# A hybrid decoder layer: in the MLP's second products, the adding transfers for product 6's weights are issued ahead of those for product 5's

## The chip, the cores and the metric

The kernel runs on one core of a Trainium2 chip. The metric is the device time of one execution in microseconds (us). The core has TensorE (PE) for matrix products, VectorE (DVE), ScalarE (ACT) and GpSimd (POOL) for the rest, and SyncE (SP), which issues transfers. Sixteen DMA engines carry out all transfers. Those that SyncE issues (queue q1) are plain copies here; those that GpSimd issues (queue q0) can add what they read to what already stands in the destination.

## The reference, cut to what matters

One decoder layer on 512 tokens of width 1024: two token mixers side by side (windowed attention and a convolution module), and behind them an MLP. The change lies in the MLP alone:

```python
hmid = jnp.square(jax.nn.relu(rms_norm(x, norm_mlp_g[l]) @ w_ff1[l]))   # 512 x 1024 @ 1024 x 4096
x = x + hmid @ w_ff2[l]                                                  # 512 x 4096 @ 4096 x 1024
```

Inputs and outputs are float32.

## The kernel before, in words

The 4096 hidden units are cut into four quarters of 1024. Each quarter has a stage of first products (the normed input by a quarter of `w_ff1`) and a stage of second products (the squared result by a quarter of `w_ff2`), so the MLP has eight stages, `ph` 0 to 7, and the second products are the odd ones. In the profile they begin at 478.66, 557.30, 633.61 and 709.92 us.

A stage multiplies 2 x 2 blocks by a scheme with seven block products in place of eight, numbered 1 to 7. In a second stage TensorE takes them in the order 1, 7, 6, 2, 5, 4, 3 (`ORDER`). Each is 24 matmuls (L1190) into the bank `ps_z`, `ps_y` or `ps_x`: products 1, 6, 5 and 3 go to `ps_z`, 7 and 4 to `ps_y`, 2 to `ps_x`.

The weights of a product are a 512 x 512 block, or a sum or difference of blocks. They come in two halves (`h` 0 and 1) of 256 rows, 512 KB each, and each half goes through these steps:

- `fetch` (L1128): a plain transfer on SyncE's queue into one of four buffers, `block0` to `block3`.
- `piece_hi` (L1153): ScalarE rounds the half to a high piece, `pieceh`.
- `piece_lo` (L1156): VectorE subtracts that from the half, which gives the low piece, `piecel`. A product is high by high, high by low and low by high, three matmuls for each tile. There are four pieces of each kind, used in turn.
- `fetch_add` (L1132): some products need the block of an earlier product plus another block. Once both pieces of a half have been made, GpSimd issues a transfer that adds the other block into the same buffer. In a second stage product 5's weights are product 1's plus a block (buffer `h11`), product 6's are product 7's plus a block (buffer `ht`), and product 4's are product 6's plus another (again `ht`). That makes six adding transfers in a stage.

`row_add` (L1195) on VectorE adds the finished bank to the running output, and `op_hi` (L1224), `op_lo` (L1228) and `op_sum` (L1233 to L1238) make the operands from the squared result.

The order on each engine is written out by hand: `at(pos, fn, ...)` gives every step a position, all steps are sorted by it, and each engine and each queue works through its own part in that order. The positions count in units of a quarter of a product, from `m`, the start of a stage. A position sets the order alone; when a step runs is set by what it waits for.

Of the kernel before, what the change touches and what calls it, by code (L numbers as in the profile page):

```python
# [53 lines left out]
def tile_hybrid_block(  # L54
# [295 lines left out]
    def at(pos, fn, *args):  # L350
        events.append((pos, len(events), fn, args))
# [755 lines left out]
    def homes(ph):  # L1107


        w, x, y, z = 0, 1, 2, 3  # L1110
        for _ in range(ph // 2):
            w, x, y, z = y, w, z, x
        return (w, x, y, z) if ph % 2 == 0 else (w, z, x, x)

    def home(ph, prod):
        return homes(ph)[{1: 0, 5: 0, 7: 1, 6: 1, 4: 1, 3: 2, 2: 3}[prod]]
# [51 lines left out]
    def halves(ph, j, t):  # L1168

        return [slice(c, c + 256) for c in (0, 256)] if (ph, j, t) == (PHASES - 1, 6, 1) else [slice(0, S)]  # L1170
# [115 lines left out]
    for ph in range(PHASES):  # L1286
        m = M0 + 28 * ph
        order = ORDER[ph]
        ff1 = ph % 2 == 0
        h11, ht, h22, h21 = homes(ph)  # L1290
# [18 lines left out]
        for j, prod in enumerate(order):  # L1309
            p = m + 4 * j  # L1310
            for h in range(2):
                n = 2 * (7 * ph + j) + h
                s, lo = p - 5.9 + 2 * h, 0.75
                if ph == 0 and j < 2:
                    s, lo = ((W0 + 5.6, 0.75), (W0 + 8.2, 0.75), (W0 + 21.8, 1.1), (W0 + 22.6, 4.5))[n]
                elif ph == 0 and (prod, h) == (5, 1):
                    lo = 0.85
                elif ph == 0 and (prod, h) == (4, 0):
                    s = p - 4.88
                elif ph == 0 and (prod, h) == (4, 1):  # L1320
                    s = p - 3.8
                elif not ff1 and prod == 7:
                    s = m - 2.95 + 2 * h
                elif not ff1 and prod == 6:
                    s = p - 3.4 + 2 * h
                at(s, piece_hi, n, home(ph, prod), h)
                at(s + lo, piece_lo, n, home(ph, prod), h)
                for t in range(2):
                    for cols in halves(ph, j, t) if h else (slice(0, S),):
                        at(p + 2 * h + t, products, ph, prod, n, h, t, cols)  # L1330
                d = s + 0.9
                if ff1:
                    if prod == 5:
                        at(d, fetch, ph + 1, h11, 0, 0, h)
                    elif prod == 4:
                        at(d, fetch, ph + 1, ht, 1, 0, h)
                elif prod == 1:
                    at(d, fetch_add, ph, h11, 0, 1, h)
                elif prod == 7:
                    at(d, fetch_add, ph, ht, 0, 0, h)  # L1340
                elif prod == 6:
                    at(d, fetch_add, ph, ht, 1, 0, h)
                elif prod == 2:
                    at(d, fetch, ph, h21, 1, 1, h)
                elif ph + 1 < PHASES:
                    at(d, fetch, ph + 1, home(ph, prod), *{5: (0, 1), 4: (1, 1), 3: (1, 0)}[prod], h)
            for t in range(2):
                e = p + 3.1 + t
                if ff1:
                    if prod in (1, 7, 6):  # L1350
                        at(e, c_copy, {1: 0, 7: 3, 6: 2}[prod], ph, prod, t)
                    elif prod == 3:
                        at(e, relu_of, 1, ph, prod, t, -1.0)
                    else:
                        at(e, c_add, {2: 0, 5: 3, 4: 2}[prod], ph, prod, t)
                else:
                    half_t, half_n, minus, store = {1: (0, 0, 0, 0), 7: (1, 1, 1, 0), 6: (1, 0, 0, 0), 2: (0, 0, 0, 1),
                                                    5: (1, 1, 1, 1), 4: (1, 0, 0, 1), 3: (0, 1, 1, 1)}[prod]
                    for part in halves(ph, j, t):
                        at(e, row_add, ph, half_t, half_n, prod, t, minus, store, part)  # L1360
            if ff1 and prod in (2, 5, 4):
                i, scale = {2: (0, 1.0), 5: (3, -1.0), 4: (2, 1.0)}[prod]
                late = 7.6 if ph == 0 and prod == 2 else 0
                at(p + (5.1 if prod == 4 else 4.9) + late, relu, i, scale)
                at(p + 5.5 + late, square_of, i)
            elif ff1 and prod == 3:
                at(p + 4.8, square_of, 1)
# [200 lines left out]
```

## Time and profile before

| what | value |
|---|---|
| median of 3 runs | 754.54 us (753.19 to 754.95) |
| the profiled execution's own time | 754.11 us |
| its span, first to last instruction | 752.3 us |
| TensorE busy | 744.9 us, 99% of the span |
| VectorE, ScalarE, GpSimd busy | 611.8, 445.0, 270.2 us |
| granted TensorE clock | 1.0 |
| adding transfers on GpSimd (L1132) | 34 of 512 KB, median 8.4 us from issue to landing |
| plain transfers of MLP weights on SyncE (L1128) | 64 of 512 KB, median 6.0 us |

A row of the timeline gives start, duration, engine, line, operation, the tile written and the tiles read, the count of merged instructions (x), and in brackets how long the engine stood idle before it and what ended that. A row of the stage windows gives the stretch, its length, then the busy time of PE, PEld (weight load), DVE, ACT and POOL, each with its count of instructions, the granted clock, the mean busy share of the DMA engines and GB/s. The chain of waits is the work that ended last, followed back from the end; its rows are start, duration and what. DMA lines give a queue's packets, MB and the time of its packets as a share of the sixteen engines' time in that stretch.

### The profile page before, as it was taken

The numbers are of one execution on the slowest core, as the hardware profiler recorded it, in microseconds if no ns is written. First come the engines' busy times: TensorE is split into PE (matmuls) and PEld (weight loads), VectorE is DVE, ScalarE is ACT, GpSimd is POOL, SyncE is SP. The second block draws the span as 40 slices with busy tenths as digits, with TensorE's granted clock in tenths as the row PEclk, the third lists the DMA queues.
The fourth block names the chain that finished last, engine by engine and source line by source line (L and its number), as shares of the span: only waits on it lengthen the run. The fifth ranks groups of instructions, "written<-read, shape, count | busy, mean of one in ns | idle before, by whom it ended". The sixth has DMA issues, their size and how long they took to land.

```text
span 752.3 us, 11423 instructions
## 1 busy us (share of the span) xinstructions
PE 744.9 (99%) x4338; PEld 652.9 (87%) x4338; DVE 611.8 (81%) x935; ACT 445.0 (59%) x709; POOL 270.2 (36%) x213
## 2 busy tenths in 40 slices
PE   8999999999999999999999999999999999999998
PEld 7889998898888888888888899978998899889986
DVE  7939998889978888878347679899779977998786
ACT  7645467667576656348225467764675467646751
POOL 0365788948666555534440002210121012101210
PEclk9999999999999999999999999999999999999999
DMA  8521131304132131623319107972598359834772
GB/s 321 196 98 43 56 114 57 109 33 140 56 124 75 57 104 65 213 68 112 111 59 332 59 29 132 247 198 96 149 215 202 108 138 218 197 121 116 171 162 112
DMA packets 64903, 97.99 MB, mean 130 GB/s; under 512 B 3104, under 2 KB 34384, under 8 KB 64848
## 3 DMA queue, kind: packets, MB, share of 16 engines
q1 hardware_dynamic: 55600, 79.44, 31.3%
q0 software_dynamic: 9248, 17.83, 13.5%
q8 instruction: 34, 0.56, 0.3%
q14 instruction: 21, 0.17, 0.1%
HBM read 95.13 MB, written 2.12 MB: 129 GB/s over the span
## 4 chain that ended last, share of the span: by engine, by line
PE 92%; DMA 3%; DVE 2%; issue 1%; ACT 1%; POOL 0%; SPq 0%; DVEq 0%; POOLq 0%; ACTq 0%
PE ps_z L1190 11%; PE ps_x L1185 9%; PE ps_y L1190 5%; PE ps_y L1185 4%; PE ps_x L1190 3%; PE ps_kv L1386 3%; PE ps_z L1185 2%; PE ps_g L502 2%; PE ps_q L192 2%; DMA block<-in_w_ff_dram 2%; PE ps_q L194 2%; PE ps_q L193 2%; PE ps_a L502 2%; PE ps_ta L502 2%; PE ps_g L504 2%; PE ps_a L504 2%
## 5 line engine op out<-in xcount | busy, mean ns | idle before, releaser
L1153 ACT CAST pieceh<-block 128x1024 fp32r<-128x1024 f32 x112 | 115.8, 1049 | 75.4 <-DMA block<-in_w_ff_dram 19.9
L1156 DVE TENSOR_TENSOR piecel<-block,pieceh 128x1024 fp32r<-128x1024 f32 x112 | 135.6, 1219 | 27.7 <-ACT pieceh L1153 27.6
L811 DVE SCALAR_TENSOR_TENSOR cv<-h,wcol,cv 128x512 f32<-128x512 f32 x208 | 146.1, 746 | 0.5
L1132 POOL DMA_DIRECT2D block<-in_w_ff_dram x34 | 41.4, 1248 | 290.7 <-DMA block<-in_w_ff_dram 148.3
L1185 PE MATMUL ps_x<-xSh,pieceh 128*128 128x256 f32 x192 | 53.0, 276 | 0.0
L1185 PE MATMUL ps_x<-xSl,pieceh 128*128 128x256 f32 x192 | 53.0, 276 | 0.0
L1185 PE MATMUL ps_x<-xSh,piecel 128*128 128x256 f32 x192 | 53.0, 276 | 0.0
L719 ACT ACTIVATE s<-s,negm 128x257 f32<-128x257 f32 (+1 forms) x64 | 30.4, 478 | 15.8 <-DVE negm L711 15.8
L1190 PE MATMUL ps_z<-piecel,aSh 128*128 128x512 f32 (+1 forms) x98 | 38.2, 390 | 1.0 <-DVE piecel L1156 1.0
L1190 PE MATMUL ps_z<-pieceh,aSh 128*128 128x512 f32 (+1 forms) x98 | 37.9, 386 | 0.4 <-ACT pieceh L1153 0.4
L1190 PE MATMUL ps_z<-pieceh,aSl 128*128 128x512 f32 (+1 forms) x98 | 37.7, 385 | 0.0
L1146 DVE TENSOR_TENSOR block<-block,block 128x1024 f32<-128x1024 f32 x30 | 36.5, 1221 | 0.8 <-DMA block<-in_w_ff_dram 0.4
L192 PE MATMUL ps_q<-wh_q,uTh 128*128 128x256 f32 x128 | 36.5, 286 | 0.0
L803 POOL TENSOR_TENSOR side<-side,tap 128x512 f32<-128x512 f32 x24 | 31.1, 1296 | 15.1 <-ACT tap L802 15.1
L194 PE MATMUL ps_q<-wh_q,uTl 128*128 128x256 f32 x128 | 36.2, 283 | 0.0
L193 PE MATMUL ps_q<-wl_q,uTh 128*128 128x256 f32 x128 | 36.2, 283 | 0.0
L1185 PEld LDWEIGHTS ps_x<-xSh,pieceh 128*128 128x128 f32 x192 | 36.0, 188 | 0.0
L1185 PEld LDWEIGHTS ps_x<-xSl,pieceh 128*128 128x128 f32 x192 | 36.0, 188 | 0.0
L1185 PEld LDWEIGHTS ps_x<-xSh,piecel 128*128 128x128 f32 x192 | 36.0, 188 | 0.0
L743 DVE TENSOR_TENSOR pTl<-ptp,pTh 128x512 fp32r<-128x512 f32 x28 | 19.1, 687 | 18.0 <-ACT pTh L739 18.0
L728 POOL TENSOR_TENSOR s<-s,r 128x1024 f32<-128x1024 f32 (+1 forms) x16 | 26.9, 1684 | 16.5 <-DVE r L723 16.5
L1224 ACT CAST aSh<-c 128x1024 fp32r<-128x1024 f32 x16 | 16.9, 1053 | 22.7 <-DVE c L1238 11.4
(332 smaller groups left out, 2501.6 us busy)
## 6 DMA issues: line engine op xcount, KB each, us to landing
block<-in_w_ff_dram SPq DMA_DIRECT2D x64, 512.0 KB, 6.0
block<-in_w_ff_dram POOLq DMA_DIRECT2D x34, 512.0 KB, 8.4
raw_g<-in_w_in_dram SPq DMA_DIRECT2D x8, 512.0 KB, 4.5
raw_a<-in_w_in_dram SPq DMA_DIRECT2D x8, 512.0 KB, 4.4
raw_q<-in_w_in_dram SPq DMA_DIRECT2D x8, 512.0 KB, 4.0
raw_ta<-in_w_in_dram SPq DMA_DIRECT2D x8, 512.0 KB, 3.9
raw_tc<-in_w_in_dram SPq DMA_DIRECT2D x8, 512.0 KB, 3.9
raw_wo<-in_w_attn_o_dram SPq DMA_DIRECT2D x8, 512.0 KB, 4.0
```

The source lines that it names most:

```text
L192: pe.matmul(ps, ah, wh, start=first, stop=False)
L193: pe.matmul(ps, ah, wl, start=False, stop=False)
L194: pe.matmul(ps, al, wh, start=False, stop=last)
L502: pe.matmul(ps, wh[:, k, :], ah(k), start=(k == 0), stop=False)
L803: ge.tensor_tensor(out=side[ct], in0=side[ct], in1=tap, op=ALU.add)
L811: ve.scalar_tensor_tensor(out=cps[ct], in0=src, scalar=w, in1=cps[ct], op0=ALU.mult, op1=ALU.add)
L1132: ge.dma_start(tl["raw"][buf][:, ks, :], block(ph, i, j)[:, ks, :], accum_op=ALU.add)
L1146: ve.tensor_tensor(out=o, in0=a, in1=b, op=ALU.add)
L1153: se.copy(piece("h", n), tl["raw"][buf][:, 2 * h:2 * h + 2, :])
L1156: ve.tensor_tensor(out=piece("l", n), in0=tl["raw"][buf][:, 2 * h:2 * h + 2, :], in1=piece("h", n).bitcast(F32), op=ALU.subtract)
L1185: pe.matmul(o, b[:, c, w], a[:, k, :], start=(first and c + q + i == 0), stop=(k == 3 and i == 2), skip_group_check=True)
L1190: pe.matmul(acc[:, cols], a[:, k, w], b[:, c, cols], start=(first and c + i == 0), stop=(k == 3 and i == 2), skip_group_check=True)
```

## The change

One position is another. Before, the adds for product 5 (called at product 1, half 0 and 1) stood 0.9 units behind the cast of product 1's half, at `m - 5.0` and `m - 3.0`; those for product 6 (called at product 7) stand at `m - 2.05` and `m - 0.05`, and those for product 4 (called at product 6) at `m + 5.5` and `m + 7.5`. Now product 5's stand at `m + 1.0` and `m + 1.05`.

```diff
                 elif prod == 1:
-                    at(d, fetch_add, ph, h11, 0, 1, h)
+                    at(m + 1.0 + 0.05 * h, fetch_add, ph, h11, 0, 1, h)
                 elif prod == 7:
                     at(d, fetch_add, ph, ht, 0, 0, h)
                 elif prod == 6:
                     at(d, fetch_add, ph, ht, 1, 0, h)
```

GpSimd in the first quarter's second stage, before (-) and after (+). Here `block0` is `h11` (product 1's and then 5's) and `block3` is `ht` (product 7's, then 6's, then 4's); DMASW and DMAHW are the semaphores of GpSimd's and SyncE's transfers.

```order
-L1132 DMA block0_4026<-in_w_ff2_dram 128x2x512 [waits DMAHW1_49,DVE_49]
-L1132 DMA block0_4026<-in_w_ff2_dram 128x2x512 [waits DMAHW2_49,DVE_49]
 L1132 DMA block3_4137<-in_w_ff2_dram 128x2x512 [waits DMASW2_49,DVE_49]
 L1132 DMA block3_4137<-in_w_ff2_dram 128x2x512 [waits DMASW3_49,DVE_49]
-L1132 DMA block3_4137<-in_w_ff2_dram 128x2x512 [waits DMASW6_49,DMASW0_49,DVE_49]
-L1132 DMA block3_4137<-in_w_ff2_dram 128x2x512 [waits DMASW7_49,DMASW1_49,DVE_49]
+L1132 DMA block0_4026<-in_w_ff2_dram 128x2x512 [waits DMAHW1_49]
+L1132 DMA block0_4026<-in_w_ff2_dram 128x2x512 [waits DMAHW2_49]
+L1132 DMA block3_4137<-in_w_ff2_dram 128x2x512 [waits DMASW4_49,DMASW0_49,DVE_49]
+L1132 DMA block3_4137<-in_w_ff2_dram 128x2x512 [waits DMASW5_49,DMASW1_49,DVE_49]
```

Product 5's two stood first and now stand third and fourth; product 6's two go from third and fourth to the front, and product 4's two stay fifth and sixth. The wait of product 5's adds for VectorE is gone, since what they wait for lies ahead of what product 6's wait for.

VectorE in the same stage, where it makes the low pieces of products 6 (`block3`), 2 (`block1`) and 5 (`block0`):

```order
 L1195 TENSOR_TENSOR x_1_3377<-x_1_3377,ps_z_4355 128x512 [waits PE_49]
-L1156 TENSOR_TENSOR piecel_4154<-block_4137,pieceh_4153 128x1024 [waits DMASW6_49,Activation_49]
+L1156 TENSOR_TENSOR piecel_4154<-block_4137,pieceh_4153 128x1024 [waits DMASW4_49,Activation_49]
 L1156 TENSOR_TENSOR piecel<-block_4027,pieceh 128x1024 [waits DMAHW3_49,Activation_49]
 L1195 TENSOR_TENSOR x_2_3379<-x_2_3379,ps_y_4352 128x512 [waits PE_49]
-L1156 TENSOR_TENSOR piecel_4176<-block_4137,pieceh_4175 128x1024 [waits DMASW7_49,Activation_49]
+L1156 TENSOR_TENSOR piecel_4176<-block_4137,pieceh_4175 128x1024 [waits DMASW5_49,Activation_49]
```

No instruction of VectorE moves; only the semaphores are others, since the transfers' numbers follow their order of issue. The same holds for ScalarE and SyncE, and TensorE's order is unchanged.

## The prediction

> **What bounds the kernel now.** I read the page's engine line first, then TensorE's waits, the chain of waits, the stage windows, and last the transfers behind the one wait that the chain shows.
>
> ```profile
> span 752.3 us, 11423 instructions
> PE 744.9 (99%) x4338; PEld 652.9 (87%) x4338; DVE 611.8 (81%) x935; ACT 445.0 (59%) x709; POOL 270.2 (36%) x213
> ...
> PE ps_z L1190 <- DVE piecel L1156: 1.0, 2, 0.8
> PE ps_z L1190 <- ACT pieceh L1153: 0.4, 1, 0.4
> ```
>
> TensorE is busy 99% of the span, so a change of the order of transfers can gain only where TensorE waits. From 478 us on its only waits are these two lines: matmuls of the second products (L1190) that wait for a weight piece. The next two views show where. The chain is in order of time (start, us, what).
>
> ```profile
> 483.30 9.00 DMA block<-in_w_ff_dram
> ...
> 492.33 1.06 ACT pieceh L1153
> ...
> 494.69 2.79 PE ps_z L1190 x11
> ...
> 568.35 5.44 PE ps_z L1190 x24
> ...
> 720.98 5.82 PE ps_z L1190 x24
> ```
>
> After 494.69 the chain is TensorE alone until 748.6, so whatever is saved ahead of it reaches the end, unless something else becomes late. The transfer in front is an adding one, issued by GpSimd at 483.30. It brings the second half of product 6's weights in the first quarter's second stage. TensorE's own rows there:
>
> ```profile
> 489.33 0.39 PE L1190 MATMUL ps_y<-pieceh,aSl 128*128 128x512 f32 x1
> 490.16 0.51 PE L1190 MATMUL ps_z<-pieceh,aSh 128*128 128x512 f32 x1 [0.44 <-ACT pieceh L1153]
> 491.42 0.50 PE L1190 MATMUL ps_z<-piecel,aSh 128*128 128x512 f32 x1 [0.76 <-DVE piecel L1156]
> ...
> 494.69 0.50 PE L1190 MATMUL ps_z<-piecel,aSh 128*128 128x512 f32 x1 [0.23 <-DVE piecel L1156]
> ```
>
> 489.33 is the last matmul of product 7 (ps_y), 490.16 the first of product 6 (ps_z). In a run without a wait 24 of them take 5.44, so their starts are 0.227 apart: product 6 should begin at 489.56. The idle figures in brackets (1.43) are less than the loss, since a pipelined matmul lasts 0.39 but its successor normally starts after 0.227. The loss is read from whole stages instead, the first quarter's second products and the second quarter's, first matmul to first matmul of what follows:
>
> ```profile
> 478.66:519.08 40.42, 38.99 (x171) 31.38 (x169) 37.06 (x39) 22.85 (x25) 6.08 (x5) 1.00 0.77 184
> 557.30:595.39 38.09, 38.09 (x170) 31.54 (x169) 36.14 (x38) 22.64 (x24) 4.84 (x4) 1.00 0.79 188
> ```
>
> The granted clock is 1.00 in both, the work is the same, and the first is 40.42 - 38.09 = **2.33** longer. The chain's 720.98 row (5.82 against 5.44 at 568.35) gives a second loss: product 6 of the fourth quarter, **0.38**. The second quarter's row is at the full pace, and nothing is to be gained there.
>
> **Why product 6's weights are late.** GpSimd's rows of that stage, then the time from issue to landing of the first, third and fourth of them, of the sixth, and of the third add of the fourth quarter:
>
> ```profile
> 476.82 1.21 POOL L1132 DMA_DIRECT2D block<-in_w_ff_dram  x1 [14.48 <-DVE piecel L1156]
> 479.15 2.44 POOL L1132 DMA_DIRECT2D block<-in_w_ff_dram  x2 [1.12 <-DVE piecel L1156]
> 483.30 1.22 POOL L1132 DMA_DIRECT2D block<-in_w_ff_dram  x1 [1.72 <-issue]
> 491.78 1.21 POOL L1132 DMA_DIRECT2D block<-in_w_ff_dram  x1 [7.25 <-DVE piecel L1156]
> 495.05 1.20 POOL L1132 DMA_DIRECT2D block<-in_w_ff_dram  x1 [2.05 <-DVE piecel L1156]
> ```
> ```profile
> L1132 POOL DMA_DIRECT2D block<-in_w_ff_dram x1: 1213/1213/1213, 476.8 to 476.8; - x1
> DMA to landing us min/median/max: 6.2/6.2/6.2
> ...
> L1132 POOL DMA_DIRECT2D block<-in_w_ff_dram x1: 1307/1307/1307, 480.3 to 480.3; - x1
> DMA to landing us min/median/max: 8.7/8.7/8.7
> ...
> L1132 POOL DMA_DIRECT2D block<-in_w_ff_dram x1: 1222/1222/1222, 483.3 to 483.3; - x1
> DMA to landing us min/median/max: 9.0/9.0/9.0
> ...
> L1132 POOL DMA_DIRECT2D block<-in_w_ff_dram x1: 1203/1203/1203, 495.0 to 495.0; - x1
> DMA to landing us min/median/max: 8.4/8.4/8.4
> ...
> L1132 POOL DMA_DIRECT2D block<-in_w_ff_dram x1: 1203/1203/1203, 710.0 to 710.0; - x1
> DMA to landing us min/median/max: 8.7/8.7/8.7
> ```
> ```profile
> q0 software_dynamic: 978, 1.89, 107.9%
> ...
> q1 hardware_dynamic: 55600, 79.44, 31.3%
> ```
>
> The first two adds (476.8, 479.15) are product 5's, the third and fourth (480.3, 483.30) product 6's, the last two product 4's. Landings: 483.0, 489.0 and 492.3 for the first, third and fourth, so about 3.0 per add behind the first. The q0 line is GpSimd's queue from 480 to 490: 107.9% of the 16 DMA engines' time, full, with these adds alone. (The q1 line, SyncE's plain transfers over the whole span, gives 0.313 x 752.3 x 0.524 / 79.44 = 1.55 per 512 KB, wanted below.) So product 6's two stand in a saturated queue behind two that are wanted three products later.
>
> **The change part by part.** It removes and adds no instruction: per second stage two adds of product 5 move behind two of product 6 on GpSimd, and on no other queue. What GpSimd waits for is made by VectorE, and what is waited for by ScalarE:
>
> ```profile
> 477.57 2.35 DVE L1156 TENSOR_TENSOR piecel<-block,pieceh 128x1024 fp32r<-128x1024 f32 x2
> 481.02 1.22 DVE L1156 TENSOR_TENSOR piecel<-block,pieceh 128x1024 fp32r<-128x1024 f32 x1
> 486.96 1.28 DVE L1195 TENSOR_TENSOR x<-x,ps_z 128x512 f32<-128x512 f32 x2
> 490.14 2.36 DVE L1156 TENSOR_TENSOR piecel<-block,pieceh 128x1024 fp32r<-128x1024 f32 x2 [1.91 <-ACT pieceh L1153]
> ```
> ```profile
> 489.06 1.99 ACT L1153 CAST pieceh<-block 128x1024 fp32r<-128x1024 f32 x2 [3.28 <-DMA block<-in_w_ff_dram]
> 494.24 2.00 ACT L1153 CAST pieceh<-block 128x1024 fp32r<-128x1024 f32 x2
> 499.62 1.05 ACT L1153 CAST pieceh<-block 128x1024 fp32r<-128x1024 f32 x1
> 503.53 1.05 ACT L1153 CAST pieceh<-block 128x1024 fp32r<-128x1024 f32 x1 [0.96 <-DMA block<-in_w_ff_dram]
> ```
>
> *Product 6, first half.* Its add must follow the low piece of product 7's first half, which ends at 479.92 (477.57 + 2.35); the issue at 480.3 cannot come earlier. What goes is the queue: as first it should take the first row's 6.2 and land at 486.5, not 489.0. The cast then ends at 487.6. VectorE, in its fixed order, is at row sums until 488.24 (486.96 + 1.28) and makes the low piece by 489.4. TensorE wants the high piece at 489.56 and the low one in its second matmul, 489.79: in time by 0.3.
>
> *Second half.* The low piece it follows ends at 482.24; the issue comes about 0.4 later (as at 480.3), at 482.7 instead of 483.30, and the landing 3.0 after the first, at 489.5 instead of 492.3. The cast ends at 490.6. VectorE has the pair of low pieces until 490.6 (488.24 + 2.36), a row sum of 0.6 (half of 1.28), then this one by 492.4. TensorE wants it 13 matmuls in, at 492.5. In time by 0.1, so the whole 2.33 goes.
>
> *Fourth quarter.* The third add, 710.0 + 8.7 = 718.7 today, should land at 716.2; only 0.38 is needed. I take all of it.
>
> *Product 5's adds.* Issued behind, at 483.9 and 485.1 (or once the first has landed, 486.5: the 1.72 of "issue" ahead of 483.30 ends 0.3 after the first landing, as if three could be in flight), they land third and fourth, at 492.5 and 495.5. Today the casts that read them are the second of the pair at 494.24 (held by a piece buffer of product 6) and 499.62; 2.33 earlier they are 492.9 and 497.3. Cover 0.4 and 1.8, and TensorE does not use product 5 before 500.4 (502.8 now). Cost nothing; without the cover VectorE's subtraction would be late first, and from 498.1 TensorE.
>
> *Product 4's adds* stay fifth and sixth, now close behind product 5's: 498.5 and 501.5, plus 1.55 for one plain transfer that shares the engines, 503.1 for the last. Today it is 495.05 + 8.4 = 503.4, and ScalarE waited 0.96 for it without harm. TensorE uses that half from 508.6 (eleven half products of 2.72 after 478.66), so with 1.05 and 1.22 for the two pieces it may land at 506.3. Cost nothing, with a margin of 3.2.
>
> The other stages with second products have no wait to lose, and the stages between issue no add of these two kinds. Unknown ends: from none of it (0) to all (2.71); I take all, since each step has a row and only the 0.3 and 0.1 of cover are thin.
>
> Sum against the profiled execution: 754.11 - 2.33 - 0.38 = 751.40. The median of the runs stands 0.43 higher at 754.54, which would give 751.83; I say **751.6**.
>
> **The rivals.** (a) *Only a part goes.* If the landings come 1 us later than worked out, or VectorE's order holds the pieces, the thin covers break: half the loss, 754.11 - 1.3 = 752.8. The 0.66 that GpSimd's issue was held, and fourth landings of 9.0, speak for such scatter; the bare 6.2 speaks against it.
>
> (b) *No gain, 754.1.* That holds if an add does not wait for those ahead of it, so that its landing is its own latency and its issue time, which hardly moves, decides. The 6.2 against 8.7 and 9.0 and the full engines speak against it. The Trainium skill ("DMA: Bandwidth & Descriptors", section "Anatomy of one DMA — SWDGE (gpsimd) path") fits such a transfer as 2.0 us plus bytes over 436 GB/s; for 512 KB that is an estimate of 3.2 us, by which adds 1.2 to 3.3 apart would not queue and the time stay at 754.1. By that fit the trace does not agree: no add here lands under 6.
>
> (c) *Slower: product 4's second half comes late*, because product 5's transfers push it back. Landing after 506.3 decides, that is 3.2 later than I have it, or 0.5 more per add in the row of six. Each us past that is 1 us of TensorE in each of four stages: at one us 754.11 - 2.71 + 4 = 755.4. Against it: the queue's work is the same, and the gap in which it has nothing to do, from the landing at 492.3 to the start of product 4's, is filled.
>
> **How the numbers follow.** Forecast 0.70 (750.4 to 752.6: the sum's two bases, and 0.9 either way for the scatter of the runs, which spread over 1.76); (a) 0.16, (b) 0.08, (c) 0.06. The range 750.4 to 753.8 takes in the forecast and (a). About 0.2%, 1.5 us, is what a measurement can tell from no change. Faster by more: the forecast and a third of (a), 0.75; within: the rest of (a), (b) and a little of (c), 0.20; slower 0.05.
>
> **What would show it.** Right: in the first quarter's second stage the first add lands 6.2 after 480.3, ScalarE's cast for product 6 starts near 486.5, no bracketed wait stands on TensorE at product 6, the stage lasts 38.1, and the fourth quarter's product 6 takes 5.44. Wrong: casts of product 6 still near 489 with no add ahead (b); a stage of 39 with the wait on VectorE (a); a wait of TensorE at products 5 or 4 in every second stage (c).

## The result, and the profile after

| | before | after |
|---|---|---|
| median of 6 runs each | 754.54 us (753.19 to 755.84) | 751.11 us (750.89 to 751.40) |
| ratio | | 0.9955, 95% interval 0.9942 to 0.9968 |
| profiled execution, its span | 754.11, 752.3 | 751.19, 749.4 |

The change makes the kernel 3.4 us (2.4 to 4.4) faster. The forecast was 751.6 with a range of 750.4 to 753.8. The runs also lie closer together: 0.5 us from lowest to highest, where before it is 2.65.

The page's first lines and TensorE's waits, after:

```profile
span 749.4 us, 11421 instructions
PE 743.6 (99%) x4338; PEld 653.0 (87%) x4338; DVE 611.8 (82%) x935; ACT 445.5 (59%) x709; POOL 270.0 (36%) x213
...
PE warm L210 <- PEq L1550: 0.8, 1, 0.8
PE ps_kv L1386 <- DVE roots L1398: 0.7, 1, 0.7
PE ps_kv L1386 <- ACT gates L330: 0.6, 1, 0.6
```

The two lines on `ps_z` are gone, and what is left lies at the kernel's start. The four stages of second products, each from its first matmul to the first of what follows (the last to its last bank): first the third and fourth before (the first two stand in the prediction), then all four after.

```profile
633.61:671.70 38.09, 38.09 (x170) 31.53 (x169) 36.10 (x38) 22.64 (x24) 4.84 (x4) 1.00 0.76 188
709.92:742.96 33.04, 33.04 (x147) 26.88 (x145) 30.31 (x32) 19.38 (x21) 4.82 (x4) 1.00 0.67 148
```
```profile
478.43:516.52 38.09, 38.09 (x170) 31.54 (x169) 36.74 (x39) 22.75 (x24) 7.29 (x6) 1.00 0.81 195
554.74:592.84 38.10, 38.10 (x171) 31.54 (x169) 36.40 (x38) 22.77 (x24) 7.29 (x6) 1.00 0.81 193
631.06:669.15 38.09, 38.09 (x170) 31.53 (x169) 36.40 (x38) 22.75 (x24) 7.29 (x6) 1.00 0.81 194
707.37:740.02 32.65, 32.65 (x146) 27.03 (x145) 30.85 (x32) 19.54 (x21) 7.27 (x6) 1.00 0.76 161
```

The first is 2.33 shorter, the last 0.39, the others are equal. That is 2.72 of the span's 2.93; the rest, 0.2, lies ahead of the MLP's second products (478.66 against 478.43). Why, GpSimd's rows and the time from issue to landing of its first two adds in the first quarter, after:

```profile
479.30 1.21 POOL L1132 DMA_DIRECT2D block<-in_w_ff_dram  x1 [17.19 <-DVE piecel L1156]
481.66 2.44 POOL L1132 DMA_DIRECT2D block<-in_w_ff_dram  x2 [1.15 <-DVE piecel L1156]
485.74 1.22 POOL L1132 DMA_DIRECT2D block<-in_w_ff_dram  x1 [1.64 <-DMA block<-in_w_ff_dram]
```
```profile
L1132 POOL DMA_DIRECT2D block<-in_w_ff_dram x1: 1213/1213/1213, 479.3 to 479.3; - x1
DMA to landing us min/median/max: 6.1/6.1/6.1
...
L1132 POOL DMA_DIRECT2D block<-in_w_ff_dram x1: 1203/1203/1203, 481.7 to 481.7; - x1
DMA to landing us min/median/max: 6.6/6.6/6.6
```

Product 6's two adds, now first, take 6.1 and 6.6 and land at 485.4 and 488.3. Before, third and fourth, they took 8.7 and 9.0. Product 5's two, now third and fourth, take 10.2 and 10.0.

Not all of this is the queue. The first add lands 3.6 sooner than before (485.4 against 489.0): 2.6 of that is the shorter way from issue to landing, and 1.0 is an earlier issue (479.30 against 480.3), because the low piece that it follows ended at 478.93 in place of 479.92. In the first quarter this issue comes 0.85 to 1.7 us after the stage's start in every profile with the same room for descriptors, in either order, so the earlier issue here is in part the luck of one execution. In the other three quarters the issues stand 0.1 and 3.3 after the stage's start in both orders (once, in a profile of before, the second at 4.0), and there the way to landing alone differs: 7.2 to 9.2 in three profiles of before, 6.0 to 6.3 after.

ScalarE and TensorE, after:

```profile
485.49 1.05 ACT L1153 CAST pieceh<-block 128x1024 fp32r<-128x1024 f32 x1 [0.64 <-DMA block<-in_w_ff_dram]
...
503.66 1.05 ACT L1153 CAST pieceh<-block 128x1024 fp32r<-128x1024 f32 x1 [2.93 <-DMA block<-in_w_ff_dram]
```
```profile
489.10 0.39 PE L1190 MATMUL ps_y<-pieceh,aSl 128*128 128x512 f32 x1
489.33 0.39 PE L1190 MATMUL ps_z<-pieceh,aSh 128*128 128x512 f32 x1
489.55 0.39 PE L1190 MATMUL ps_z<-piecel,aSh 128*128 128x512 f32 x1
```

The cast of product 6 starts at 485.49 where it started at 489.06, and TensorE goes from product 7 (`ps_y`) to 6 (`ps_z`) at its pace of 0.23. The lateness has been passed on: ScalarE now waits 1.42 for product 5's first half and 2.93 for product 4's second (0.96 before). TensorE waits for neither: the stage lasts 38.09.

### The profile page after: what moved, and what is told of

The parts are those of the page before. It is cut to its first block, busy times and chain, and to the rows that moved or that the text cites. A ratio compares the mean times of both kernels' runs of the same rounds, so it can differ in the third digit from the quotient of the medians.

```text
span 749.4 us, 11421 instructions
## 1 busy us (share of the span) xinstructions
PE 743.6 (99%) x4338; PEld 653.0 (87%) x4338; DVE 611.8 (82%) x935; ACT 445.5 (59%) x709; POOL 270.0 (36%) x213
## 4 chain that ended last, share of the span: by engine, by line
PE 98%; DMA 1%; ACT 0%; SPq 0%; DVE 0%; DVEq 0%; issue 0%
PE ps_x L1185 12%; PE ps_z L1190 12%; PE ps_y L1190 6%; PE ps_y L1185 6%; PE ps_z L1185 3%; PE ps_x L1190 3%; PE ps_kv L1386 3%; PE ps_g L502 2%; PE ps_q L192 2%; PE ps_q L194 2%; PE ps_q L193 2%; PE ps_a L502 2%; PE ps_ta L502 2%; PE ps_g L504 2%; PE ps_a L504 2%; PE ps_g L503 2%
## 5 line engine op out<-in xcount | busy, mean ns | idle before, releaser
L1190 PE MATMUL ps_z<-piecel,aSh 128*128 128x512 f32 (+1 forms) x98 | 37.7, 385 | 0.0
L1190 PE MATMUL ps_z<-pieceh,aSh 128*128 128x512 f32 (+1 forms) x98 | 37.7, 385 | 0.0
L1190 PE MATMUL ps_z<-pieceh,aSl 128*128 128x512 f32 (+1 forms) x98 | 37.7, 385 | 0.0
L470 POOL TENSOR_TENSOR wl_wo<-raw_wo,wh_wo 128x1024 fp32r<-128x1024 f32 x8 | 19.8, 2479 | 25.2 <-ACT wh_wo L466 25.2
```

The source lines that it names most:

```text
L1190: pe.matmul(acc[:, cols], a[:, k, w], b[:, c, cols], start=(first and c + i == 0), stop=(k == 3 and i == 2), skip_group_check=True)
```

## The experiments

The edits are all to the line that the change touches, unless shown otherwise. Times of one group of runs are compared with runs of the kernel before on the same chip.

**The change in one part of the quarters.**

```diff
+at(m + 1.0 + 0.05 * h if ph == 1 else d, fetch_add, ph, h11, 0, 1, h)    # first quarter alone
+at(d if ph == 1 else m + 1.0 + 0.05 * h, fetch_add, ph, h11, 0, 1, h)    # the three others
```

> The change in the first quarter's second products alone. Theory (product 6's adds stood behind product 5's in a full queue, and TensorE felt it in the first quarter by 2.33 us and in the fourth by 0.38): 2.3 us and more come off, the first quarter's stage lasts 38.1, product 6 of the fourth quarter still takes about 5.8. Rival (the gain is spread over all four stages, or comes from ahead of the MLP): about a quarter of the change's gain, under 1 us.

> The change in the second to fourth quarters, the first as before. Theory: only the fourth quarter's 0.38 us comes off, the first quarter's stage stays at about 40.4. Rival (gain spread over the stages): three quarters of it, some 2 us.

Measured: 752.70 for the first quarter alone, ratio 0.9976 (0.9965 to 0.9986), so 1.8 us (1.1 to 2.6); 753.38 for the others, 0.9984 (0.9972 to 0.9996), 1.2 us (0.3 to 2.1). The gains add up to about the whole. The even spread, under 1 us for the first quarter, falls; but both intervals still take in the theory's 2.3 and 0.38, and the second takes in the rival's 2 as well, so the times alone do not tell how the gain is shared. The runs of both spread over some 3 us (751.26 to 754.15, and 752.05 to 755.13), as before's do. The profile with the first quarter changed says more. A wait stands in the third quarter, where the first profile of before had none (38.51 against 38.09):

```profile
631.33:669.84 38.51, 38.51 (x171) 31.38 (x170) 35.77 (x37) 22.20 (x24) 4.84 (x4) 1.00 0.80 186
```

And in its first quarter product 6's adds were issued at 480.19 and 482.50, nearly where the forecast had them (480.3 and 482.7). They took 6.3 and 7.5, and the stage lasted 38.26, so 0.17 was still lost there: the forecast's thin cover did not hold in this execution. With the three others changed, the first quarter's stage still lasts 40.09 and the others lose nothing. So the loss per quarter had to be looked at in more than one execution.

**The kernel before, two more profiles.**

> The kernel before, word for word, for a second profile of it. Theory: the ratio is 1, and the wait at product 6 of the first quarter is there again but of another length (1 to 4 us), since the runs of before spread over 2.65 us and those of the change over 0.5. Rival: the wait is 2.33 as before, and the spread of before comes from ahead of the MLP.

> The kernel before once more, for a third profile. Theory (in each quarter the wait at product 6 is what the slowest DMA engine of one add leaves over a slack of some 0.5 us, and so another in each execution): waits at product 6 in one to four of the quarters, 1 to 5 us in all, other lengths than in the first two profiles. Rival (a fixed loss): the first quarter's stage 40.4 and the fourth quarter's 0.4 again.

Measured: ratio 1.0005 (0.9994 to 1.0016) for the first of them, one time of 755.65 for the second. The four stages in each:

```profile
477.78:517.07 39.29, 38.54 (x170) 31.38 (x169) 36.23 (x38) 22.16 (x24) 5.79 (x5) 1.00 0.79 188
555.29:594.49 39.20, 38.44 (x171) 31.46 (x170) 35.84 (x37) 22.18 (x24) 4.84 (x4) 1.00 0.77 183
632.70:671.48 38.78, 38.53 (x171) 31.39 (x169) 35.74 (x37) 22.18 (x24) 4.84 (x4) 1.00 0.76 185
709.70:742.83 33.13, 33.10 (x147) 26.87 (x146) 30.32 (x32) 19.38 (x21) 4.82 (x4) 1.00 0.70 147
```
```profile
478.42:518.97 40.55, 38.82 (x171) 31.39 (x170) 36.53 (x38) 22.46 (x24) 6.08 (x5) 1.00 0.79 182
557.18:595.85 38.67, 38.54 (x170) 31.39 (x169) 35.75 (x37) 22.19 (x24) 4.84 (x4) 1.00 0.78 185
634.07:673.06 38.99, 38.54 (x171) 31.39 (x169) 35.75 (x37) 22.20 (x24) 4.84 (x4) 1.00 0.75 184
711.28:744.50 33.22, 33.09 (x147) 26.88 (x145) 30.31 (x32) 19.37 (x21) 4.82 (x4) 1.00 0.69 146
```

Less 38.09 (and 32.65 for the last), the same program loses in its four quarters

| profile of before | first | second | third | fourth | sum |
|---|---|---|---|---|---|
| the one that the forecast used | 2.33 | 0.00 | 0.00 | 0.39 | 2.72 |
| second | 1.20 | 1.11 | 0.69 | 0.48 | 3.48 |
| third | 2.46 | 0.58 | 0.90 | 0.57 | 4.51 |

The mean is 3.6, and the change takes 3.4. A fixed loss, the rival of both, falls: the second quarter loses 0.00, 1.11 and 0.58.

The losses can be set against the landings. For each stage, the landings of product 6's first and second half in us after the stage's start:

| profile | first | second | third | fourth |
|---|---|---|---|---|
| before, the one that the forecast used | 10.33, 13.64 | 7.96, 10.47 | 8.02, 10.54 | 8.78, 11.48 |
| before, second | 9.60, 12.11 | 7.89, 12.42 | 9.09, 11.62 | 8.87, 11.40 |
| before, third | 10.85, 13.39 | 8.98, 11.52 | 9.29, 11.80 | 8.96, 11.50 |
| after | 6.99, 9.85 | 6.38, 9.46 | 6.17, 9.42 | 6.25, 9.32 |

Take 8.40 as the latest landing that costs nothing for the first half (9.60 - 1.20, second profile) and 11.31 for the second (13.64 - 2.33, first profile). Then a stage's loss is the greater of the two delays, and nothing where neither is late. For the third profile's third quarter, 9.29 - 8.40 is 0.89 and 11.80 - 11.31 is 0.49, and the stage lost 0.90. These two limits were read off afterwards, from two stages; they give the loss of all 36 stages in nine profiles (these four and those of five experiments, from the first quarter alone to less room for descriptors, without the one with the adds behind product 4's) within 0.03. So what these stages lose is the lateness of these two adds and nothing else. Take its loss away from each execution of before, and 751.39, 750.49 and 751.14 are left, about where the change runs (750.89 to 751.40).

What scatters is the landing of single adds. Product 6's second add in the second quarter was issued at 560.57 in the first profile and took 7.2; in the second profile it was issued at 558.57, as long after its stage's start, and took 9.1. What the DMA engines did at its end, in that second profile:

```profile
L1132 POOL DMA_DIRECT2D block<-in_w_ff_dram x1: 1222/1222/1222, 558.6 to 558.6; - x1
DMA to landing us min/median/max: 9.1/9.1/9.1
...
565.00:566.00 1.00, 1.00 (x6) 0.81 (x6) 1.00 (x2) 0.26 (x1) 0.02 (x1) 1.00 0.22 37
566.00:567.00 1.00, 1.00 (x6) 0.84 (x5) 1.00 (x2) 0.00 (x0) 1.00 (x1) 1.00 0.07 12
```

The last two columns are the busy share of the 16 engines and GB/s. From 566 to 567 the share is 0.07, about one engine of 16. The trace has sixteen marks of completion for each add: fifteen of this one's came by 566.0, the last at 567.7, and that is where the add counts as landed. In the first profile this add landed 0.84 ahead of its limit and product 6's first half 0.44, so 2 us more of one engine reached TensorE; the new order's landings in that quarter, 6.38 and 9.46, leave about 2 and 1.9. Why one engine ends late is not known.

**Only the second of product 5's adds goes behind.**

```diff
+at(m + 1.05 if h else d, fetch_add, ph, h11, 0, 1, h)
```

> Only the second of product 5's two adds moves behind product 6's; the first keeps its place at the front. Theory: the first add is nearly through when product 6's first is issued (476.8 + 6.2 = 483.0 against 480.3 + 3 before its data move), so product 6's land within 0.5 us of where the full change puts them and all waits go: the time of the full change within 0.3 us, while product 4's second half lands nearer to the 1 us wait of before than to the 3 us of the full change. Rival (any add ahead costs its 3.0 us): about half of the gain, 1.4 us.

Measured: 751.05, ratio 0.9957 (0.9945 to 0.9970), all stages at 38.1 (the last at 32.65), the same as the full change; its five runs lie between 750.57 and 751.44. Product 6's adds are issued at 479.3 and 481.6 and land at 485.5 and 488.6, product 4's second half at 500.7 instead of 503.6. So the add that hurt is the second; the first, issued 3.5 us ahead of product 6's, costs them little (6.3 and 7.0 from issue to landing). The rival, 3.0 us for any add ahead, falls. Moving the first alone was not run. This version has the same time and more room at product 4.

**Product 5's adds left out.**

```diff
+pass
```

> The order before, with product 5's adds left out altogether, so that product 5 uses product 1's weights. Theory (nothing but the two adds ahead in the queue made product 6's late): product 6's land as in the change, no wait on TensorE, 751.1 (750.7 to 751.5), and no further gain from the 8 fewer adds. Rival (the change's gain comes from the other waits and semaphores of the new order): 754.2, as before, or a part of it.

Measured: 751.20, ratio 0.9962 (0.9949 to 0.9974), runs from 750.62 to 751.44, all stages at 38.1 (the last at 32.65). Product 5 then multiplies product 1's weights, so this is not the layer's result. As expected: to have nothing ahead of product 6's adds is worth the same as to have them first, and the eight transfers cost nothing that can be measured where they now stand.

**Product 5's adds behind product 4's too.**

```diff
+at(m + 8.0 + 0.05 * h, fetch_add, ph, h11, 0, 1, h)
```

> Product 5's adds go one step further, behind product 4's (fifth and sixth in GpSimd's order). This looks for the price of rival (c): adds that come after they are wanted. Theory (the queue serves in order of issue, about 3.0 us each): product 5's are issued near 494 in the first quarter, land near 502 and 505, and TensorE wants them at 498.1 and 500.8: about 4 us of wait in each of the four stages, 751.1 + 16 = 767 (761 to 770). Rival (an add's landing is its own 6.1 us): landing near 500 and 501, 1 to 2 us in each stage, about 757.

> The kernel with product 5's adds behind product 4's once more, for a profile: its timed runs gave 791.6 us, 24 more than the theory's 767, and the profile taken with them was of an execution in which TensorE itself ran at under half pace throughout. Theory: the adds land as the queue serves them, near 502 and 505, and the rest is what their lateness sets off: ScalarE and SyncE work in a fixed order, so casts and fetches behind product 5's casts come late as well, and TensorE waits at product 5, 4 and 3 of each stage and in the stage behind, 10 us per quarter. Rival: the adds themselves land far later than the queue explains (over 12 us from issue).

Measured: 791.22, median of three executions (790.62 to 792.03), ratio 1.0495 (1.0476 to 1.0515), and 791.17 with the second profile. An execution ahead of these took 2657.32, with matmuls of the second products (L1190) at 1.08 in the mean, where they take 0.39 before; why is not known, and it is left out of the median. The others are slower than the change as expected, but by 40 us and not 16. Their profile: the landing, ScalarE, VectorE, TensorE, and the stretch of product 5 in the first quarter.

```profile
492.62 10.92 DMA block<-in_w_ff_dram
...
503.64 1.04 ACT L1153 CAST pieceh<-block 128x1024 fp32r<-128x1024 f32 x1 [11.54 <-DMA block<-in_w_ff_dram]
...
504.72 1.23 DVE L1156 TENSOR_TENSOR piecel<-block,pieceh 128x1024 fp32r<-128x1024 f32 x1 [9.25 <-ACT pieceh L1153]
505.86 1.22 DVE L1228 TENSOR_TENSOR aSl<-c,aSh 128x1024 fp32r<-128x1024 f32 x1
507.00 1.27 DVE L1195 TENSOR_TENSOR x<-x,ps_z 128x512 f32<-128x512 f32 x2
...
507.82 0.77 PE L1190 MATMUL ps_z<-pieceh,aSh 128*128 128x512 f32 x1 [7.38 <-DVE x L1195]
...
507.82:515.71 7.89, 7.89 (x24) 6.32 (x25) 7.89 (x9) 4.21 (x5) 0.00 (x0) 0.68 0.54 175
```

The add lands at 503.5, 1.5 later than the theory had it, and 10.9 from issue: the rival, over 12, falls. The second expectation was wrong in its own theory too: it had TensorE wait at products 5, 4 and 3, and it waits at product 5 alone, once in each stage. Two things make the rest. TensorE does not wait for the weights but for `x<-x,ps_z`: product 5 uses the bank in which product 6 stands, the row sum that empties it lies behind product 5's low piece in VectorE's fixed order, and so 4.3 us pass from landing to TensorE, not 2.3. And after a wait of 7.4 the granted clock is down (0.68 in the mean over product 5), and its 24 matmuls take 7.89 in place of 5.44. Both happen in all four stages: the waits cost 7.5 to 8.1 each and the lower clock 1.5 to 3.0 (product 5 at 7.89, 7.23, 6.95 and 8.40), 40 together.

**Less room for GpSimd's descriptors, in the order before.**

```diff
-dynamic_dma_scratch_size=2048
+dynamic_dma_scratch_size=1536
```

> The kernel before with three quarters of the room that the program gives GpSimd for its transfer descriptors (1536 in place of 2048). Theory (that room lets three adds be in flight; the queue, not the issue, sets the landings): the third add of a stage is now issued 0.3 us after the first has landed, 3 us later than before, and the fourth after the second; their landings move by under 1 us, and the time by 0 to +2. Rival (the room has nothing to do with the 1.72 us of idle ahead of the fourth add): the issue times stay.

Measured: 757.54, ratio 1.0051 (1.0032 to 1.0070), so 3.8 us slower where 0 to 2 was expected. The issue times came as the theory has them:

```profile
475.87 1.20 POOL L1132 DMA_DIRECT2D block<-in_w_ff_dram  x1 [10.11 <-DVE piecel L1156]
478.26 1.22 POOL L1132 DMA_DIRECT2D block<-in_w_ff_dram  x1 [1.19 <-DVE piecel L1156]
482.88 1.21 POOL L1132 DMA_DIRECT2D block<-in_w_ff_dram  x1 [3.40 <-DVE aSl L1228]
```
```profile
L1132 POOL DMA_DIRECT2D block<-in_w_ff_dram x1: 1203/1203/1203, 475.9 to 475.9; - x1
DMA to landing us min/median/max: 6.7/6.7/6.7
...
L1132 POOL DMA_DIRECT2D block<-in_w_ff_dram x1: 1213/1213/1213, 482.9 to 482.9; - x1
DMA to landing us min/median/max: 6.1/6.1/6.1
```

The third add starts 0.3 after the first has landed (475.87 + 6.7 = 482.57), and so do the third and fourth of every quarter after the first and second. It then takes 6.1, about what the first add of a second stage takes before (6.0 to 6.5, once 7.5), so in this quarter it lands where it did in the first profile, at 489.0. What failed in the expectation is the landings: in the other three quarters the second halves land 1.1 to 2.0 later than in the first profile, not under 1. That is 12.2 to 12.6 after the stage's start, past the limit of 11.31, and the first halves, at 9.0 to 9.2, are past theirs. The four stages lose 2.08, 0.91, 1.30 and 1.29, 5.6 in all.

## Why the prediction was right

- *What bounds it, and where the loss sits.* Right: product 6 of the first and fourth quarter gave 2.33 and 0.39, against 2.33 and 0.38 forecast, and no wait came in their place. That every loss of the nine profiles follows from the landings of product 6's two adds confirms it.
- *The queue.* Right, and shown from three sides: the adds put behind, one of them put behind, or both left out give 751.1, 751.05 and 751.2. Product 6's adds landed 6.1 and 6.6 from issue as the first in the queue, where 6.2 and 6.8 were taken (issue at 482.7, landing at 489.5).
- *The thin covers of 0.3 and 0.1.* They came out at 1.1 and 1.0, because the adds were issued 1.0 sooner than in the profile of before. That was luck of this execution in good part. "The issue at 480.3 cannot come earlier" held for the profile that was read, not for the next; with the first quarter alone changed the issue was at 480.19, and 0.17 was lost.
- *Product 5's and 4's adds.* Landings of 492.6, 495.8 and 503.6 stand against 492.5, 495.5 and 503.1, and they cost nothing, as forecast. One step there was wrong without a price: TensorE was given until a landing at 498.1. By the profile with product 5's adds behind product 4's, the row sum stands in between, and 4.3 us pass from landing to TensorE instead of 2.3, which makes it about 496.0. The real margin is about 3.4 and not 5.6.
- *The size.* 3.4 against 2.9 from median to median. The term that was mis-sized is "nothing is to be gained" in the second and third quarters: one execution showed 0.00 there, two others 0.58 to 1.11. The 2.71 was one draw from a loss that varies between 2.7 and 4.5 in the three profiles. The time itself was hit better than the gain, since an execution less its own loss comes out near 751 each time. The sum gave 751.40 and the runs 751.11; going up to 751.6 for the median of the runs was the wrong way, because, as far as the three profiles tell, what lifts that median is more of the same waits. (The forecast's own span, said to be the two bases and 0.9 either way, is 750.5 to 752.7 by its terms, and not 750.4 to 752.6.)
- *The rivals.* (b) fell with the landings. (a), a part that stays, did not come in the change's profile, but 0.17 of it did with the first quarter alone. (c) did not come: product 4's second half landed at 503.6, with 506.3 as the limit. What an add too late costs was seen at product 5 instead, 40 us in place of 16, so a price of 1 us per us of lateness leaves out what VectorE's order adds and the lower clock after a long wait.

## What to carry to other kernels

Where transfers of one queue stand in order of issue, order them by when they are wanted, and look at the queue's own occupation (here sixteen engines fully busy from 480 to 489, with GpSimd's adds alone) before reading a late landing as latency. A transfer with under 1 us of slack can be a loss on average even where one profile shows none (here 0.44 and 0.84 of slack, and then losses of 1.11 and 0.58): take two or three profiles of the same program, and set each stage's loss against the landings. And give the latest allowed time of a step by its place in the engine that works in order, not by the product that uses its data.

## What the runs showed that was not expected

- GpSimd kept at most three adds of 512 KB in flight with 2048 for its descriptors, and two with 1536: the next one started 0.3 us after the oldest had landed (485.74 after 479.30 + 6.1 with the change, and in the same way in the three other quarters).
- One DMA engine of sixteen ended an add 1.7 us after the other fifteen (567.7 against 566.0), and the landing was its.
- Waits of 7.4 to 7.9 us on TensorE halved its granted clock (0.67 in the mean over the first of them); waits of up to 0.8 left it at 1.00 in every stage. The Trainium skill ("TensorE: Matmul & The Clock Gate", section "Part 1: The HAM clock gate (the "warmup" mystery)") has the clock fall to half after at least one idle window of about 3.4 us and return after at least one such window of sustained work. The trace agrees in kind only: the clock fell 2.2 to 4.6 us after the last matmul ahead of the four waits, once sooner than that window, and returned 3.0 to 6.1 us after product 5's start.
